# Six small-product groups on TensorE: one matmul of 128 stationary columns, or two of 64

## The chip, the cores and the metric

The kernel runs on one core of a Trainium2 chip. The metric is the device time of one execution in microseconds. The engines are TensorE (PE in the profile, its weight loads PEld), VectorE (DVE), ScalarE (ACT), GpSimd (POOL) and SyncE (SP), which issues nearly all DMAs.

## The reference

Two requests (512 and 256 tokens, width 1024) pass through two layers. In each layer, four mixers (A: grouped-query attention, B: differential attention, C: retention, D: RWKV-7 in both directions) work on one projection of the normalised input, and a SwiGLU feed-forward follows:

```python
for l in range(DEPTH):
    h = _rms(x, p['norm_mix_pre'][l])
    z = h @ p['w_in'][l]
    z_a, z_b, z_c, z_d = jnp.split(z, list(GROUP_OFFS), axis=-1)
    ...
    mix = jnp.concatenate([o_a, o_b, o_c, o_d], axis=-1) @ p['w_out'][l]
    x = x + _rms(mix, p['norm_mix_post'][l])
    h = _rms(x, p['norm_ffn_pre'][l])
    f = (jax.nn.silu(h @ p['ffn_w_gate'][l]) * (h @ p['ffn_w_up'][l])) @ p['ffn_w_down'][l]
    x = x + _rms(f, p['norm_ffn_post'][l])
```

A head is 64 wide. So the product of attention weights with values (A, B, C) has 64 output columns, and D's state is a 64 x 64 matrix for each head and direction.

## The kernel before

Every layer has a mixer phase and a feed-forward phase. The large products (input projection `zc`, `zb`, `zv`, `za`, `dz`, output projection `op`, feed-forward `fg`, `fu`, `dn`) split their operands into a high and a low part of type fp32r and take three matmuls each, with 128 stationary columns (the `lhsT` operand, loaded by LDWEIGHTS) and 256 or 512 moving columns (the `rhs` operand, streamed by MATMUL). The text below calls them the dense matmuls. The small products are plain fp32; the trace holds two MATMUL and two LDWEIGHTS records for each of these.

In the mixer phase, six streams are woven (`weave`): D's preparation and chain, the dense projections, the preparation of heads, the attention units, and the two output stages. The tile framework then orders each engine's instructions by its own timeline of the program (`schedule_with_timeline_sim`), so the order on TensorE is found by a scheduler and not written out by hand. An engine works through its instructions in that order.

These are the small products that the change touches, by the name of the PSUM tile that they write:

- `sd`, in `scores` inside `d_chain` (L537): 64 rows, 128 stationary columns, 128 moving columns. Eight matmuls in each of the 12 chain steps of a layer. The row half (`h`) decides which 64 rows of the array they use.
- `px` and `pg`, in `step_of` inside `d_chain` (L575, L592): 128 rows, 128 stationary and 64 moving columns, eight matmuls each in a chain step. Between them stands `pu` (L584), which already uses 64 rows and 64 stationary columns: rows and columns 0 to 63 for one head, 64 to 127 for the other.
- `oa` and `ob`, in `pv_mm` (L766): probabilities times values of attention A and B, 128 stationary and 64 moving columns, four (first request) or two (second request) matmuls that accumulate.
- `oc`, in `att_c` (L907): the same product for C.

For both layers together these are 192 matmuls each of `sd`, `px` and `pg`, and 160 each of `oa`, `ob` and `oc`. A chain step runs `sd`, masks on DVE, `px`, a copy on ACT (`xy`), `pu`, copies on ACT, `pg`, and state updates on DVE.

Of the kernel before, what the change touches and what calls it, by code (L numbers as in the profile page):

```python
# [19 lines left out]
P = 128  # L20
# [62 lines left out]
class Trunk:  # L83
# [71 lines left out]
    def piece(self, l, idx, n=1024, tags=("whi", "wlo")):  # L155
        nc = self.nc
        raw = self.slot("raw", [P, 1024], f"raw{l}_{idx}")
        nc.sync.dma_start(out=raw[:, :n], in_=self.wp[l, idx][:, :n])
        w = 768 if tags[0] == "D" else 1024
        hi = self.slot(tags[0], [P, w], f"whi{l}_{idx}", F32R)  # L160
        lo = self.slot(tags[1], [P, w], f"wlo{l}_{idx}", F32R)
        nc.scalar.activation(hi[:, :n], raw[:, :n], AF.Copy)  # L162
        self.nlo += 1
        eng = nc.vector if idx in FAST or self.nlo % 2 == 0 else nc.gpsimd
        eng.tensor_tensor(out=lo[:, :n], in0=raw[:, :n], in1=hi[:, :n].bitcast(F32), op=ALU.subtract)  # L165
        return hi, lo

    def tok_mm(self, ps, t, parts, ncol):

# [328 lines left out]
    def d_chain(self, l):  # L498
        nc = self.nc
        V, S, A, T = nc.vector, nc.scalar, nc.gpsimd, nc.tensor  # L500
        H = (slice(0, 64), slice(64, 128))
# [6 lines left out]
        def scores(s, step):  # L508
            t0, n, tt0, ntl, c0, nch = SEQS[s]
            nm = f"{l}_{s}_{step}"  # L510
            chunk = (c0 + step, c0 + nch - 1 - step)
            krs, bks, brs, svs = [], [], [], []
            tt = tta[:, (2 * s + step % 2)]
            for d in range(2):
                c = chunk[d]
                kt, bt = self.tmp(f"kr{nm}_{d}"), self.tmp(f"br{nm}_{d}")
                kr = kt[:, 0:512].rearrange("p (h q x) -> p h q x", h=2, q=2)
                bk = kt[:, 512:768].rearrange("p (q x) -> p q x", q=2)
                br = bt[:, 0:512].rearrange("p (h q x) -> p h q x", h=2, q=2)
                sv = bt[:, 512:768].rearrange("p (h q x) -> p h q x", h=2, q=2)  # L520
                for h in range(2):
                    nc.sync.dma_start(out=kr[H[h], h].rearrange("p q (k x) -> p q k x", k=2), in_=self.kd[d, c, H[h], :, 0:2, :])
                nc.sync.dma_start(out=bk.rearrange("p q (k x) -> p q k x", k=2), in_=self.kd[d, c, :, :, 2:4, :])
                for h in range(2):
                    nc.sync.dma_start(out=sv[H[1 - h], h],
                                      in_=self.vd[c * 64:c * 64 + 64, :].rearrange("t (q h x) -> t q h x", q=2, h=2)[:, :, h, :])
                nc.sync.dma_start(out=tt[:, d], in_=self.td[c, :, d])
                krs.append(kr)
                bks.append(bk)
                brs.append(br)  # L530
                svs.append(sv)

            psv = [self.bank("pb", f"sd{nm}_{h}").rearrange("p (d q x) -> p d q x", d=2, q=2) for h in range(2)]
            for d in range(2):
                for q in range(2):
                    for h in range(2):
                        T.matmul(psv[h][:, d, q], lhsT=bks[d][H[h], q], rhs=krs[d][H[h], h, q], start=True, stop=True)  # L537
            for d in range(2):
                for h in range(2):
                    oh, ot = H[h], H[1 - h]  # L540
                    x, y = (slice(64, 128), slice(0, 64)) if h == 0 else (slice(0, 64), slice(64, 128))
                    V.tensor_tensor(out=krs[d][ot, h], in0=psv[h][ot, d], in1=self.mask[ot, d:d + 1, :].to_broadcast([64, 2, 128]), op=ALU.mult)
                    V.tensor_tensor(out=brs[d][oh, h, :, x], in0=psv[h][oh, d, :, x],
                                    in1=self.mask[oh, d:d + 1, y].to_broadcast([64, 2, 64]), op=ALU.mult)
                    A.memset(brs[d][ot, h, :, x], 0.0)
            pt = self.bank("pb", f"bt{nm}")
            ptv = pt.rearrange("p (d q x) -> p d q x", d=2, q=2)
            for d in range(2):
                for q in range(2):
                    T.transpose(ptv[:, d, q], bks[d][:, q], self.ident)  # L550
            for d in range(2):
                S.activation(brs[d][:, 0, :, 0:64], ptv[:, d, :, 0:64], AF.Copy)
                S.activation(brs[d][:, 1, :, 64:128], ptv[:, d, :, 64:128], AF.Copy)
            return krs, brs, svs, tt

        def step_of(s, step, krs, brs, svs, tt):
            t0, n, tt0, ntl, c0, nch = SEQS[s]
            nm = f"{l}_{s}_{step}"
            ms = sta[:, s]
            msv = ms.rearrange("p (d q) x -> p d q x", q=2)  # L560
            wc = self.wc[:, c0 + max(step, 1) - 1]

            for d in range(2):
                for h in range(2):
                    if step == 0:
                        A.memset(svs[d][H[h], h], 0.0)
                    else:
                        V.tensor_tensor(out=svs[d][H[h], h], in0=msv[H[h], d], in1=wc[H[h], d].unsqueeze(2).to_broadcast([64, 2, 64]),
                                        op=ALU.mult)
            if 0 < step < nch - 1:  # L570
                A.tensor_tensor(out=msv, in0=msv, in1=wc.unsqueeze(3).to_broadcast([P, 2, 2, 64]), op=ALU.mult)
            px = self.bank("pb", f"px{nm}")
            pxv = px.rearrange("p (u x) -> p u x", x=64)
            for u, (h, d, q) in enumerate(units):
                T.matmul(pxv[:, u], lhsT=krs[d][:, h, q], rhs=svs[d][:, h, q], start=True, stop=True)  # L575
            xy = xya[:, s]
            S.activation(xy, pxv, AF.Copy)
            yield 2
            pu = self.bank("pb", f"pu{nm}")
            puv = pu[:, 0:256].rearrange("p (d q x) -> p d q x", d=2, q=2)  # L580
            for d in range(2):
                for q in range(2):
                    for h in range(2):
                        T.matmul(puv[H[h], d, q], lhsT=tt[H[h], d, q], rhs=xy[H[h], 4 * h + 2 * d + q], start=True, stop=True)  # L584
            for d in range(2):
                for h in range(2):
                    S.activation(svs[d][H[h], h], puv[H[h], d], AF.Copy)
            yield 2
            pg = self.bank("pb", f"pg{nm}")
            pgv = pg.rearrange("p (u x) -> p u x", x=64)  # L590
            for u, (h, d, q) in enumerate(units):
                T.matmul(pgv[:, u], lhsT=brs[d][:, h, q], rhs=svs[d][:, h, q], start=True, stop=True)  # L592
            yy = sta[:, 2 + s]
            for h in range(2):
                us = slice(4 * h, 4 * h + 4)
                if step == 0:
                    V.tensor_copy(out=ms[H[h]], in_=pgv[H[h], us])
                elif step < nch - 1:
                    V.tensor_tensor(out=ms[H[h]], in0=pgv[H[h], us], in1=ms[H[h]], op=ALU.add)
            for h in range(2):  # L600
                us = slice(4 * h, 4 * h + 4)
                V.tensor_tensor(out=yy[H[1 - h]], in0=pgv[H[1 - h], us], in1=xy[H[1 - h], us], op=ALU.add)
            for d, c in enumerate((c0 + step, c0 + nch - 1 - step)):
                rows = self.yd[d, c * 64:c * 64 + 64].rearrange("t (q h x) -> t q h x", q=2, h=2)
                for h in range(2):
                    nc.sync.dma_start(out=rows[:, :, h], in_=yy[H[1 - h], 2 * d:2 * d + 2])
            yield 2
# [155 lines left out]

    def pv_mm(self, po, pT, v, nt):
        for j in range(nt):
            self.nc.tensor.matmul(po, lhsT=pT[:, j * P:(j + 1) * P], rhs=v[:, j], start=j == 0, stop=j == nt - 1)  # L766

    def pieces(self, l, idx):
        return [(*self.piece(l, idx + i), range(4 * i, 4 * i + 4), 256, 0) for i in range(2)]
# [119 lines left out]
    def att_c(self, l, g, s):  # L889
        nc = self.nc  # L890
# [3 lines left out]
        w = []  # L894
        for j in range(nt):
            if j % 2 == 0:
                wt = self.slot("Q", [P, 2, 512], f"w{nm}_{j}")
            ps = self.bank("pS", f"s{nm}_{j}")
# [5 lines left out]
        po = self.bank("pO", f"o{nm}")  # L904
        for i in range(nt):
            for j in range(nt):
                nc.tensor.matmul(po[:, i * 64:i * 64 + 64], lhsT=w[j][:, i * P:(i + 1) * P], rhs=z[:, j, 128:192], start=j == 0, stop=j == nt - 1)  # L907
            if i % 2:
                yield 1.5
        pov = po[:, :nt * 64].rearrange("p (i d) -> p i d", d=64)  # L910
# [545 lines left out]
```

## Time and profile before

| | us |
|---|---|
| median of 3 runs | 2338.31 |
| lowest and highest run | 2332.1, 2345.1 |
| the profiled execution | 2336.97 |
| its span, first to last instruction | 2335.2 |
| PE busy in the span | 2246.6 (96%) |
| DVE busy in the span | 1291.8 (55%) |

All times of the trace count from the span's start. Layer 0's mixers end at about 590 us, its feed-forward at about 1160; layer 1's mixers end at about 1760 and its feed-forward closes the span. A PE group is named by line, output tile and inputs, then the part of the array that it uses (rows*columns: 128*128 is all of it, 64*128 half the rows, 64*64 a quarter), then the moving operand's shape. The duration of one MATMUL record includes its way through the array, so records overlap: the pace of a run is read from the starts, not from durations.

### The profile page before, as it was taken

How to read it: one execution, taken by the hardware profiler on the slowest of the kernel's cores; microseconds unless marked ns; L12 is line 12 of the kernel's file. 1: busy time of each engine (PE TensorE's matmuls, PEld its weight loads, DVE VectorE, ACT ScalarE, POOL GpSimd, SP SyncE). 2: the span in 40 equal slices, each digit the busy share in tenths (PEclk: the TensorE clock that was granted, in tenths of full speed). 3: DMA queues.
4: the chain of work that ended last, by engine and by line, in shares of the span. 5: the costliest groups of instructions: out<-in, count | busy, mean ns of one | idle time of the engine just before them, and what ended most of it. 6: DMA issues, size and time to landing. Idle time of an engine off the chain costs nothing.

```text
span 2335.2 us, 39824 instructions
## 1 busy us (share of the span) xinstructions
PE 2246.6 (96%) x15960; PEld 2028.8 (87%) x15960; DVE 1291.8 (55%) x2404; ACT 804.5 (34%) x1675; POOL 582.5 (25%) x521
## 2 busy tenths in 40 slices
PE   7999999999899999999999899999999999999997
PEld 7889999989888888888888799898898888888886
DVE  5598557885623333333567874678855343333345
ACT  4333335566431111221244333455654211222111
POOL 1342313325311111111233422133352111111113
PEclk9999999999999999999999899999999999999999
DMA  4543563335421111222324525633453111122112
GB/s 170 134 113 98 156 193 110 93 113 178 145 79 55 63 55 55 72 73 73 102 87 125 134 78 146 204 104 88 131 189 117 64 63 55 55 73 73 64 64 81
DMA packets 245080, 240.69 MB, mean 103 GB/s; under 512 B 138784, under 2 KB 191904, under 8 KB 244896
## 3 DMA queue, kind: packets, MB, share of 16 engines
q1 hardware_dynamic: 244896, 238.15, 33.2%
q8 instruction: 126, 2.06, 0.4%
q14 instruction: 58, 0.48, 0.1%
HBM read 183.03 MB, written 55.05 MB: 102 GB/s over the span
## 4 chain that ended last, share of the span: by engine, by line
PE 37%; DVE 7%; DMA 2%; issue 1%; ACT 1%; SPq 1%; POOL 1%; DVEq 0%; POOLq 0%; ACTq 0%
PE fg L189 8%; PE fu L189 8%; PE dn L1231 8%; PE dz L189 2%; PE op L178 2%; PE za L178 1%; PE zb L178 1%; PE pg L592 1%; DVE wlo L165 1%; PE px L575 1%; PE ob L766 1%; DMA raw<-in_wp_dram 1%; PE sd L537 1%; PE zc L178 1%; DVE nper L455 1%
## 5 line engine op out<-in xcount | busy, mean ns | idle before, releaser
L165 POOL TENSOR_TENSOR wlo<-raw,whi 128x1024 fp32r<-128x1024 f32 (+1 forms) x108 | 259.4, 2402 | 1034.9 <-ACT whi L162 854.7
L1237 DVE TENSOR_TENSOR y<-y,dn 128x512 f32<-128x512 f32 x240 | 162.7, 686 | 340.4 <-PE dn L1231 339.8
L162 ACT ACTIVATE whi<-raw 128x1024 fp32r<-128x1024 f32 (+1 forms) x222 | 225.3, 1021 | 334.3 <-DMA raw<-in_wp_dram 121.1
L189 PE MATMUL fg<-hh,whi 128*128 128x256 f32 (+1 forms) x768 | 250.4, 326 | 0.9 <-ACT hh L202 0.9
L189 PE MATMUL fg<-hl,whi 128*128 128x256 f32 (+1 forms) x768 | 250.4, 326 | 0.4 <-DVE hl L203 0.4
L189 PE MATMUL fg<-hh,wlo 128*128 128x256 f32 (+1 forms) x768 | 249.2, 325 | 0.0
L189 PE MATMUL fu<-hl,whi 128*128 128x256 f32 (+1 forms) x768 | 249.1, 324 | 0.0
L189 PE MATMUL fu<-hh,whi 128*128 128x256 f32 (+1 forms) x768 | 249.0, 324 | 0.0
L189 PE MATMUL fu<-hh,wlo 128*128 128x256 f32 (+1 forms) x768 | 248.4, 323 | 0.0
L165 DVE TENSOR_TENSOR wlo<-raw,whi 128x1024 fp32r<-128x1024 f32 (+1 forms) x114 | 154.6, 1356 | 128.8 <-ACT whi L162 127.8
L1231 PE MATMUL dn<-whi,ah 128*128 128x512 f32 x528 | 208.9, 396 | 1.9 <-DVE y L1237 1.9
L1231 PE MATMUL dn<-wlo,ah 128*128 128x512 f32 x528 | 209.4, 397 | 0.0
L1231 PE MATMUL dn<-whi,al 128*128 128x512 f32 x528 | 203.8, 393 | 0.0
L189 PEld LDWEIGHTS fg<-hh,whi 128*128 128x128 f32 x768 | 146.4, 191 | 16.1 <-ACT hh L202 1.3
L189 PEld LDWEIGHTS fg<-hl,whi 128*128 128x128 f32 x768 | 146.1, 190 | 15.1 <-DVE hl L203 1.0
L189 PEld LDWEIGHTS fu<-hl,whi 128*128 128x128 f32 x768 | 146.3, 190 | 13.6
L189 PEld LDWEIGHTS fu<-hh,wlo 128*128 128x128 f32 x768 | 146.1, 190 | 13.7
L189 PEld LDWEIGHTS fg<-hh,wlo 128*128 128x128 f32 x768 | 146.3, 190 | 13.4
L189 PEld LDWEIGHTS fu<-hh,whi 128*128 128x128 f32 x768 | 146.4, 191 | 13.1
L1219 ACT ACTIVATE ah<-th 128x768 fp32r<-128x768 f32 (+2 forms) x52 | 38.6, 742 | 297.6 <-DVE th L1217 297.6
L1197 ACT ACTIVATE th<-fg 128x512 f32<-128x512 f32 (+1 forms) x88 | 42.7, 485 | 234.8 <-PE fg L189 234.2
L1231 PEld LDWEIGHTS dn<-whi,al 128*128 128x128 f32 x528 | 98.7, 188 | 23.3
(358 smaller groups left out, 5586.6 us busy)
## 6 DMA issues: line engine op xcount, KB each, us to landing
raw<-in_wp_dram SPq DMA_DIRECT2D x184, 512.0 KB
raw<-in_wp_dram SPq DMA_DIRECT2D x38, 384.0 KB
kr<-kd SPq DMA_DIRECT2D x96, 64.0 KB
kr<-kd SPq DMA_DIRECT2D x48, 128.0 KB
x<-xm SPq DMA_DIRECT2D x24, 256.0 KB
xf<-x SPq DMA_DIRECT2D x12, 512.0 KB
gain<-in_bc_dram SPq DMA_DIRECT2D x8, 512.0 KB
bd<-sh SPq DMA_DIRECT2D x8, 512.0 KB
```

Source lines behind the costliest of these rows:

```text
L162: nc.scalar.activation(hi[:, :n], raw[:, :n], AF.Copy)
L165: eng.tensor_tensor(out=lo[:, :n], in0=raw[:, :n], in1=hi[:, :n].bitcast(F32), op=ALU.subtract)
L178: mm(ps, lhsT=a, rhs=b[:, c:c + ncol], start=i == 0, stop=i == tot - 1)
L189: mm(ps, lhsT=a, rhs=b, start=i == 0, stop=i == 3 * NK - 1)
L455: V.tensor_tensor(out=q[:, j + 1:32, 0:j], in0=q[:, j + 1:32, 0:j], in1=ev, op=ALU.add)
L537: T.matmul(psv[h][:, d, q], lhsT=bks[d][H[h], q], rhs=krs[d][H[h], h, q], start=True, stop=True)
L575: T.matmul(pxv[:, u], lhsT=krs[d][:, h, q], rhs=svs[d][:, h, q], start=True, stop=True)
L592: T.matmul(pgv[:, u], lhsT=brs[d][:, h, q], rhs=svs[d][:, h, q], start=True, stop=True)
L1197: nc.scalar.activation(th[:, c], pg[s][:, :n], AF.Tanh, scale=0.5)
L1219: nc.scalar.activation(ah[:, c], th[:, c], AF.Copy)
L1231: nc.tensor.matmul(ps, lhsT=a[p], rhs=w[q], start=i == 0, stop=i == tot - 1)
L1237: nc.vector.tensor_tensor(out=yt, in0=yt, in1=ps, op=ALU.add)
```

## The change

A new helper issues two matmuls of 64 stationary columns, the first for columns and output partitions 0 to 63, the second for 64 to 127, and the six groups call it in place of one matmul of 128 stationary columns:

```diff
+    def halves_mm(self, ps, lhsT, rhs, start=True, stop=True):
+
+        for c in (slice(0, 64), slice(64, 128)):
+            self.nc.tensor.matmul(ps[c], lhsT=lhsT[:, c], rhs=rhs, start=start, stop=stop)
...
-                        T.matmul(psv[h][:, d, q], lhsT=bks[d][H[h], q], rhs=krs[d][H[h], h, q], start=True, stop=True)
+                        self.halves_mm(psv[h][:, d, q], bks[d][H[h], q], krs[d][H[h], h, q])
...
-                T.matmul(pxv[:, u], lhsT=krs[d][:, h, q], rhs=svs[d][:, h, q], start=True, stop=True)
+                self.halves_mm(pxv[:, u], krs[d][:, h, q], svs[d][:, h, q])
...
-                T.matmul(pgv[:, u], lhsT=brs[d][:, h, q], rhs=svs[d][:, h, q], start=True, stop=True)
+                self.halves_mm(pgv[:, u], brs[d][:, h, q], svs[d][:, h, q])
...
-            self.nc.tensor.matmul(po, lhsT=pT[:, j * P:(j + 1) * P], rhs=v[:, j], start=j == 0, stop=j == nt - 1)
+            self.halves_mm(po, pT[:, j * P:(j + 1) * P], v[:, j], j == 0, j == nt - 1)
...
-                nc.tensor.matmul(po[:, i * 64:i * 64 + 64], lhsT=w[j][:, i * P:(i + 1) * P], rhs=z[:, j, 128:192], start=j == 0, stop=j == nt - 1)
+                self.halves_mm(po[:, i * 64:i * 64 + 64], w[j][:, i * P:(i + 1) * P], z[:, j, 128:192], j == 0, j == nt - 1)
```

In the built program, `px`, `pg`, `oa`, `ob` and `oc` now use the array in the form 128*64 (864 matmuls on columns 0 to 63, 864 on columns 64 to 127), and `sd` in the form 64*64. TensorE has 15108 matmuls in place of 14052. Nothing else in the program's text differs, but the scheduler lays out all engines anew.

The rows below are the order on PE, from the built programs: line, operation, output tile<-inputs, the output's partitions x elements, and how many like it follow each other. In `px_0_5` the numbers are request and chain step. The first place is layer 0, request 0, chain step 5, around `px`; before:

```order
L804 MATMUL tqa_0_0_5166<-cs,xa_0_0_4886 128x128 x4
L575 MATMUL px_0_5_4876<-br_0_5_0_4715,kr_0_5_0_4714 128x64 x2
L575 MATMUL px_0_5_4876<-br_0_5_1_4723,kr_0_5_1_4722 128x64 x2
L575 MATMUL px_0_5_4876<-br_0_5_0_4715,kr_0_5_0_4714 128x64 x2
L575 MATMUL px_0_5_4876<-br_0_5_1_4723,kr_0_5_1_4722 128x64 x2
L537 MATMUL sd_0_6_0_4927<-kr_0_6_0_4911 128x128 x2
L537 MATMUL sd_0_6_0_4927<-kr_0_6_1_4919 128x128 x2
L766 MATMUL ob_1_0_1_4894<-vb_0_3780,pTb_1_0_1_0_5070 128x64 x4
L970 MATMUL sb_1_0_1_3_0_5220<-kb_1_0_1_4515,qb_1_0_1_4514 128x512
```

The same place with the change:

```order
L183 MATMUL za_1_1_0_5787<-wlo_11_5407,hh 128x256
L171 MATMUL px_0_5_5228<-br_0_5_0_5035,kr_0_5_0_5034 64x64 x4
L171 MATMUL px_0_5_5228<-br_0_5_1_5043,kr_0_5_1_5042 64x64 x4
L171 MATMUL px_0_5_5228<-br_0_5_0_5035,kr_0_5_0_5034 64x64 x4
L171 MATMUL px_0_5_5228<-br_0_5_1_5043,kr_0_5_1_5042 64x64 x4
L171 MATMUL sd_0_6_0_5287<-kr_0_6_0_5271 64x128 x4
L171 MATMUL sd_0_6_0_5287<-kr_0_6_1_5279 64x128 x4
L764 MATMUL ptb_1_0_1_1_5609<-cs,pb_1_0_1_1_5366 128x128 x4
L975 MATMUL sb_1_0_1_3_1_5629<-kb_1_0_1_4803,qb_1_0_1_4802 128x512
```

Eight matmuls of `px` have become 16, still in one stretch, but now the form changes three times here (128*128 to 128*64, to 64*64, back to 128*128), where it changed twice (to 64*128 for `sd` and back). The second place is the retention product of head 0, request 1, in layer 0, between dense matmuls `zc`; before:

```order
L178 MATMUL zc_1_1_0_2193<-whi_16_1967,hh 128x256
L476 MATMUL pq_0_1243<-z_0_1147,nt_0_566 32x32
L178 MATMUL zc_1_1_0_2193<-wlo_16_1968,hh 128x256
L178 MATMUL zc_1_1_0_2193<-whi_16_1967,hl 128x256
L907 MATMUL oc_0_1_2219<-zc_0_1_1885,wc_0_1_0_2155 128x64 x4
L178 MATMUL zc_1_1_1_2239<-whi_15_1961,hh 128x256
```

The same place with the change:

```order
L183 MATMUL zc_1_1_0_2241<-whi_16_1999,hl 128x256
L171 MATMUL oc_0_1_2267<-zc_0_1_1917,wc_0_1_0_2203 64x64 x7
L481 MATMUL pq_0_1243<-z_0_1147,nt_0_566 32x32
L171 MATMUL oc_0_1_2267<-zc_0_1_1917,wc_0_1_0_2203 64x64
L183 MATMUL zc_1_1_1_2291<-whi_15_1993,hh 128x256
```

Four `oc` matmuls that stood among dense ones in the same form are now eight in another form, and a `pq` of a third form has moved in between. Counted over the whole order, the form changes 190 times before (94 times away from 128*128 and back, two times between other forms) and 477 times with the change (218 times away from 128*128 and back, 41 times between other forms).

## Rows read from the trace of the kernel before

**Rows 1.** The page, sections 1 and 2: busy us, and tenths in 40 slices.

```profile
span 2335.2 us, 39824 instructions
PE 2246.6 (96%) x15960; PEld 2028.8 (87%) x15960; DVE 1291.8 (55%) x2404; ACT 804.5 (34%) x1675; POOL 582.5 (25%) x521
PEclk9999999999999999999999899999999999999999
```

**Rows 2.** Stretches: length, busy us (instructions) of PE, PEld, DVE, ACT, POOL, clock, DMA.

```profile
160.00:280.00 120.00, 117.22 (x1258) 112.39 (x1257) 83.94 (x210) 42.22 (x104) 31.94 (x55) 0.97 0.42 114
280.00:470.00 190.00, 185.56 (x1615) 175.66 (x1615) 134.44 (x315) 91.93 (x257) 49.41 (x72) 0.97 0.47 137
470.00:590.00 120.00, 110.14 (x877) 105.41 (x876) 81.96 (x189) 73.72 (x185) 47.05 (x43) 0.97 0.47 154
590.00:1160.00 570.00, 563.49 (x3178) 491.81 (x3178) 221.71 (x313) 132.84 (x182) 103.61 (x49) 0.99 0.22 75
1445.00:1635.00 190.00, 184.83 (x1617) 173.30 (x1616) 138.25 (x320) 92.38 (x259) 48.68 (x72) 1.00 0.46 139
```

**Rows 3.** The chain that ended last, by line, from 1520 to 1640 us.

```profile
by line: PE za L178 28.3%; PE pg L592 9.1%; PE ob L766 8.9%; PE px L575 7.5%; PE sd L537 6.4%; PE sb L970 4.9%; PE ptb L759 4.2%; PE pu L584 3.1%; DMA raw<-in_wp_dram 2.6%; issue 2.6%; PE bt L550 1.8%; SPq L606 1.3%; PE oT L1009 1.3%; DVE s
```

**Rows 4.** PE groups by shape: records | busy us, mean ns | idle before, releaser.

```profile
L537 PE MATMUL sd<-kr 64*128 64x128 f32 x384 | 47.4, 288 | 3.0 <-DMA kr<-kd 1.3 <-PE sb L970 0.9 <-issue 0.8
L592 PE MATMUL pg<-br 128*128 128x64 f32 x384 | 46.9, 275 | 0.7 <-ACT br L587 0.7
L575 PE MATMUL px<-br,kr 128*128 128x64 f32 x384 | 46.8, 274 | 0.3 <-DVE br L568 0.3
L766 PE MATMUL oa<-za,pTa 128*128 128x64 f32 x320 | 42.6, 277 | 0.2 <-DVE ob L991 0.2
L766 PE MATMUL ob<-vb,pTb 128*128 128x64 f32 x320 | 42.5, 270 | 0.0
L907 PE MATMUL oc<-zc,wc 128*128 128x64 f32 x320 | 42.0, 270 | 1.7 <-DVE wc L901 1.2 <-DVE oc L917 0.4
```

**Rows 5.** Timeline of PE at one `px` run: start us, us from first start to last end.

```profile
260.18 1.95 PE L575 MATMUL px<-br,kr 128*128 128x64 f32 x16
261.97 0.50 PE L907 MATMUL oc<-zc,wc 128*128 128x64 f32 x3
```

**Rows 6.** Timelines of PE, then PEld, at one `pu` run between dense matmuls.

```profile
272.61 0.28 PE L178 MATMUL zb<-whi,hl 128*128 128x256 f32 x1
272.73 0.28 PE L178 MATMUL zb<-whi,hh 128*128 128x256 f32 x1
272.94 0.68 PE L584 MATMUL pu<-xy,tt 64*64 64x64 f32 x16
273.55 0.39 PE L178 MATMUL zb<-wlo,hh 128*128 128x256 f32 x1
273.77 0.28 PE L178 MATMUL zb<-whi,hl 128*128 128x256 f32 x1
...
272.93 0.55 PEld L584 LDWEIGHTS pu<-xy,tt 64*64 64x64 f32 x16
```

**Rows 7.** The `pu` records: count, duration ns min/median/max, first and last start.

```profile
L584 PE MATMUL pu<-xy,tt x384: 217/218/366, 272.9 to 1631.3; 64*64 64x64 f32 x192
L584 PEld LDWEIGHTS pu<-xy,tt x384: 129/135/228, 272.9 to 1631.3; 64*64 64x64 f32 x192
```

**Rows 8.** Timeline of PE at an `sd` run of one row half, layer 1.

```profile
1573.58 0.28 PE L178 MATMUL za<-wlo,hh 128*128 128x256 f32 x1
1573.79 1.16 PE L537 MATMUL sd<-kr 64*128 64x128 f32 x8
1574.87 0.39 PE L178 MATMUL za<-whi,hl 128*128 128x256 f32 x1
1575.10 0.33 PE L766 MATMUL ob<-vb,pTb 128*128 128x64 f32 x2
```

**Rows 9.** Timeline of PE at an `sd` run whose row halves take turns, layer 0.

```profile
371.95 1.17 PE L537 MATMUL sd<-kr 64*128 64x128 f32 x16
```

**Rows 10.** Stretches as in rows 2, where DVE is busiest.

```profile
400.00:450.00 50.00, 49.52 (x419) 46.69 (x418) 41.11 (x86) 26.94 (x71) 14.81 (x19) 1.00 0.31 88
1550.00:1600.00 50.00, 50.00 (x432) 47.48 (x433) 42.21 (x95) 28.97 (x77) 16.45 (x21) 1.00 0.26 69
```

## The prediction

> **What bounds the kernel now.** I read the totals first: PE is busy for 96% of the span, DVE for 55% [rows 1]. The table of stretches says where that holds. In the mixer stretches that contain the changed products, PE is busy 117 of 120, 186 of 190 and 110 of 120 us in layer 0, and layer 1 is alike (185 of 190 in its chain stretch) [rows 2]. The granted clock is 0.97 to 1.00 there, so nearly all of it is at 2.4 GHz, and no clock term enters the sum. The feed-forward stretch (563 of 570 us) holds none of the six groups and should stay as it is. The chain that ended last confirms that PE's queue sets the pace: from 1520 to 1640 us, `za`, `pg`, `ob`, `px`, `sd`, `sb`, `ptb` and `pu` alone make 72% of it [rows 3]. So time taken from PE in these stretches should mostly come off the end, and time added on PE comes onto it. The reader should look at the six groups next: about 42 to 47 us of busy time each, 268 us together, almost no idle time before them [rows 4]. Busy time counts overlapped pipeline ends, so the price of a matmul has to be taken from starts.
>
> **What one product costs now.** A `px` run of 16 records starts at 260.18, the next run at 261.97: 1.79 us, 112 ns a record, and 223 ns for a matmul of two records [rows 5]. `pg`, `oa`, `ob` and `oc` have the same shape and nearly the same mean and busy time per record [rows 4]. They are 192 + 192 + 3 x 160 = 864 matmuls.
>
> **What two halves cost.** No row shows the form 128*64. The nearest is `pu`: 64 stationary columns, 64 moving ones, on two quarters of the array that differ in rows and in columns [rows 6]. Its 16 records take 0.68 us; the last one lasts 0.22 [rows 7], so 15 steps take 0.46 us, 31 ns a record. Its 16 loads take 0.55 us, the last lasts 0.135, so 28 ns a load. As two quarters take turns, one quarter alone goes at 55 to 62 ns. If the two column halves of `px` work beside each other as `pu`'s quarters do, a former matmul becomes four records of 31 ns, 124 in place of 223 ns. If they go one after the other, it becomes four of about 58 ns, 232: 9 ns more than now. I take the first. What speaks for it is `sd`: where its matmuls stay on one row half, 8 records take 1.16 us [rows 8]; where the halves take turns, 16 records take 1.17 [rows 9]. So parts of the array that share all columns and differ in rows run side by side, and `pu` shows it for parts that differ in both. Parts that share all rows and differ in columns alone are what is not shown.
>
> The Trainium skill speaks on both sides here. "TensorE: Matmul & The Clock Gate", Part 3, "What overlaps and what doesn't", says that a load overlaps running matmuls only when the row group differs; by that the halves of `px` would go in turn and the first term of the sum would be a loss of 8 us. "TensorEngine Tiling (Array Packing)", "Key Properties", says that different tiles load and multiply in parallel, columns included; by that it is the gain taken below. The trace bears out the first page's condition for rows and has no case of columns alone.
>
> **First term:** 864 x (223 - 124) = 86 us less on PE.
>
> **Second term, the changes of form.** A run in another form than its neighbours is not free. Dense matmuls start every 0.12 us. Around `pu`, from the last dense start before (272.73) to the second dense start after (273.77) there are 1.04 us; two dense steps are 0.24 and 16 records are 0.50, so 0.30 us are left for going over and back [rows 6]. (The second start counts, because the first dense matmul after it is recorded at 273.55 and yet holds the next one up by 0.22.) Around the `sd` run the same reckoning gives 1575.10 - 1573.58 = 1.52, less 0.24, less 8 x 0.112: 0.38 us [rows 8]. I take 0.34 for a trip to 128*64 and back, and half of it, 0.17, for a direct change between two other forms. Before, none of the 864 matmuls paid this, since they had the dense form. The order has 218 trips in place of 94 and 41 direct changes in place of two: 124 x 0.34 + 39 x 0.17 = 42 + 7 = 49 us more on PE. By the ends it is 43 to 54 us.
>
> So a run must be long enough to earn its trip. Eight former matmuls (`px`, `pg`) gain 0.79 us and pay 0.34. Four (`oa`, `ob` of the first request) gain 0.40. Two (`oa`, `ob` of the second request, pieces of `oc`) gain 0.20, a loss.
>
> **Third term, `sd`.** Each record still streams 128 moving columns, so its 112 ns stay [rows 8]; the halved load was hidden under that. 192 matmuls become 768 records of which two at least run at once: 43 us, as if all 384 records went singly now. If four quarters run at once, 21 us. Before, some runs already had two row halves at once [rows 9] and most did not. I take 4 us less, with 15 less and 7 more as ends. The masks on DVE, the memsets on POOL, the copies on ACT and all DMAs are the same in number and size. Their cover is the dense matmuls beside them, which stay, and no wait is added.
>
> **Sum.** -86 + 49 - 4 = -41 us of work on PE, about 20 in each layer's mixers. Not all comes off the end: the chain steps pass through ACT and DVE between `px`, `pu` and `pg`, and DVE is at 41 to 42 us of 50 where the attention units run [rows 10]. I let 6 us go there: -35. Against the profiled execution of 2336.97 us (span 2335.2, 1.8 us around it) that is 2302; the median of the runs stands 1.3 us higher, so I say 2303. With trips at 0.30, `sd` at -15 and nothing lost, it is -58 (2280); with trips at 0.38, `sd` at 0 and half lost, it is -16 (2322). These are the forecast's own ends.
>
> **Rivals.**
>
> *The halves go one after the other (slower).* Place: the 128*64 runs. Then the first term is +8 us, the trips remain at +49, and `sd`'s column halves in turn cost 0 to +43, depending on how much its row halves overlap. That is +57 to +100, 2396 to 2438, around 2410. It decides from a pace of 42 ns a record on: 864 x (223 - 4 x 42) is 48 us, just what the trips take. For it: no row shows columns alone side by side, and both halves read the same 128 partitions, for weights and for moving data. Against it: `pu` and `sd` show independent work in every other pairing [rows 6, 9]. Chance 0.18.
>
> *PE gets shorter, the end does not.* DVE at 84% and the chain's latencies take the bound, and the scheduler's new order may open waits of its own. -41 us on PE would turn into idle time before PE's instructions, and the time would be 2327 to 2340. For it: the DVE rows [rows 10]. Against it: PE is at 96% and most of the chain is PE [rows 2, 3]. Chance 0.11.
>
> *Changes between 128*128 and 128*64 are free.* Both `pu` and `sd` change the number of rows too, so their price might not hold for columns alone. Then the 49 us fall away: -90, or 2250. For it nothing but the missing row; against it, both known changes cost 0.30 or more [rows 6, 8]. Chance 0.06.
>
> That the change doesn't do what it says is ruled out as far as the program goes: the built order holds the 1728 matmuls of 128*64.
>
> **How the numbers follow.** Forecast 0.65, the rivals 0.18, 0.11 and 0.06. A measurement of this kernel can tell about 0.5%, 12 us, from no change. Faster by more than that (below 2327): the forecast and the free changes, 0.70, leaving 0.01 of the forecast's far end. Within it: that 0.01 and the second rival, 0.12. Slower: the first rival, 0.18. The range goes from the free changes (2250) to a little above the second rival (2345); left out are the first rival and about 0.02 on the low side.
>
> **What would show it.** A `px` run would have 32 records of the form 128*64 in about 1.0 us, and the chain's `xy` copies would come about 0.8 us sooner after the first `px`; if it takes 1.9 us, the first rival holds. From the last dense start before a 128*64 run to the second after it, 0.3 to 0.4 us should remain when the dense steps and the records are taken off; 0 would be the third rival. `sd` runs of 16 records or more would take no longer than 112 ns for each pair. The stretches from 590 to 1160 and from 1760 on would keep their length, and the mixer phases would each be 15 to 20 us shorter, with PE still at 94% or more; if PE's share falls below that at an unchanged length, it is the second rival. A time above 2345 would mean that the halves do not share the array, and one below 2280 that trips are cheaper, or `sd` far better, than I read.

## The result and the profile after

The changed kernel takes 2308.68 us in the median (2306.99 to 2315.69), the kernel before 2338.8 beside it. The ratio is 0.9877, with a 95% interval from 0.9842 to 0.9912: faster by 1.2%, 30 us, where 35 were forecast (2303, range 2250 to 2345). The profiled execution took 2307.11 us.

The page of the changed kernel, sections 1 and 2, to be read beside [rows 1]:

```profile
span 2305.3 us, 44071 instructions
...
PE 2195.2 (95%) x18072; PEld 1940.4 (84%) x18072; DVE 1278.9 (55%) x2404; ACT 803.9 (35%) x1675; POOL 577.7 (25%) x521
...
PEclk9999999999999999999999999999999999999999
```

PE is busy 2195.2 us in place of 2246.6, so 51.4 less; the span fell by 29.9. The difference, 21.5 us, is new idle time on PE (110.1 in place of 88.6). So the work got cheaper by more than forecast, and less of that reached the end. The clock bears little on this pair: the mean granted clock is 0.979 before and 0.981 after, which is 97 and 89 us at 1.2 GHz, worth at most 4 us of the 51.4.

The phases say where. A mixer phase ends where the feed-forward's first `fg` starts. The two mixer phases of the kernel before, then of the changed kernel, in the columns of [rows 2]:

```profile
0.00:597.60 597.60, 562.76 (x4853) 528.18 (x4854) 416.05 (x905) 276.81 (x668) 180.69 (x206) 0.97 0.46 137
1159.20:1756.40 597.20, 566.30 (x4876) 529.13 (x4875) 426.36 (x890) 272.66 (x660) 195.45 (x211) 0.97 0.44 129
```

```profile
0.00:585.20 585.20, 537.29 (x5909) 484.58 (x5910) 413.85 (x905) 276.32 (x667) 181.16 (x205) 0.97 0.48 140
1145.50:1728.70 583.20, 543.25 (x5932) 486.48 (x5931) 417.55 (x889) 272.55 (x661) 192.70 (x211) 0.96 0.46 132
```

The mixers are 12.4 and 14.0 us shorter, with 25.5 and 23.1 us less PE work; PE's share fell from 94 and 95% to 92 and 93%. Of the 29.9 us, 26.4 came off the mixers and 3.5 off the two feed-forward phases, whose work is the same.

The groups of the changed kernel, which answer to [rows 4]:

```profile
L171 PE MATMUL sd<-kr 64*64 64x128 f32 x768 | 40.3, 281 | 7.2 <-DMA kr<-kd 4.1 <-ACT xy L582 1.4 <-issue 1.0
L171 PE MATMUL ob<-vb,pTb 128*64 128x64 f32 x640 | 31.1, 229 | 0.5 <-ACT pTb L766 0.5
L171 PE MATMUL oa<-za,pTa 128*64 128x64 f32 x640 | 29.7, 232 | 1.2 <-ACT pTa L766 0.9
L171 PE MATMUL oc<-zc,wc 128*64 128x64 f32 x640 | 29.1, 234 | 0.0
L171 PE MATMUL px<-br,kr 128*64 128x64 f32 x768 | 28.0, 224 | 1.2 <-DVE br L573 1.2
L171 PE MATMUL pg<-br 128*64 128x64 f32 x768 | 27.9, 225 | 0.0
```

Twice as many records, and each 128*64 group is busy 28 to 31 us in place of 42 to 47. The timeline of PE in the changed kernel, a `pg` and a `px` run between dense matmuls, and another `px` run with the copy on ACT that waits for it:

```profile
384.50 0.28 PE L183 MATMUL za<-wlo,hh 128*128 128x256 f32 x1
384.70 1.15 PE L171 MATMUL pg<-br 128*64 128x64 f32 x32
385.68 1.10 PE L171 MATMUL px<-br,kr 128*64 128x64 f32 x32
386.72 0.38 PE L183 MATMUL za<-whi,hl 128*128 128x256 f32 x1
386.94 0.28 PE L183 MATMUL za<-whi,hh 128*128 128x256 f32 x1
```

```profile
262.84 1.15 PE L171 MATMUL px<-br,kr 128*64 128x64 f32 x32
...
264.04 0.60 ACT L582 ACTIVATE xy<-px 128x512 f32<-128x512 f32 x1 [0.90 <-PE px L171]
```

From 384.50 to 386.94 there are 2.44 us; less two dense steps of 0.12, 2.20. Runs of 4, 8, 16, 32 and 64 records between dense matmuls in this trace leave 0.46, 0.57, 0.81, 1.27 and 2.21 us by the same reckoning: a straight line of 0.34 us and 29.2 ns a record. So the halves work beside each other (29 ns, not 58), and the trip costs 0.34. The copy `xy` starts 1.20 us after the first `px`. Before, it started 1.99 us after a `px` at 260.18 [rows 5]:

```profile
262.17 0.60 ACT L577 ACTIVATE xy<-px 128x512 f32<-128x512 f32 x1 [1.62 <-PE px L575]
```

What PE waited for in the changed kernel's layer 0 chain stretch, 280 to 470 us (who waits, for whom: us in total, times, longest), largest first, and then the two largest of the kernel before in the same stretch:

```profile
PE tb L940 <- POOL zb L733: 3.9, 1, 3.9
PE ptb L764 <- DVE pb L981: 3.0, 1, 3.0
...
PE tb L940 <- DVE sl L943: 2.3, 1, 2.3
```

```profile
PE ptb L759 <- DVE sl L938: 2.0, 1, 2.0
PE bt L550 <- DVE br L543: 1.1, 1, 1.1
```

The work on DVE, ACT and POOL in the mixers is nearly unchanged (842, 549 and 376 us before, 831, 549 and 374 after), PE has less to do in between, and waits for their results. The waits listed are of that kind; whether an earlier arrival or the new order makes each of them is not separated here. The chain that ended last, 1495 to 1600 us, has more of DVE and POOL in it than before. Added up over all its lines, of which the view shows the first, PE holds 67%, DVE 19% and POOL 6%; in the same stretch of the kernel before they hold 90, 3 and 0%:

```profile
by line: PE za L183 28.0%; PE sd L171 7.4%; PE ob L171 6.6%; PE ptb L764 5.9%; PE pg L171 5.0%; PE sb L975 4.6%; DMA fb<-yd 4.1%; PE px L171 4.0%; PE pu L589 2.4%; issue 2.3%; DVE kr L547 2.2%; POOL ra L151 2.2%; POOL rb L151 2.0%; PE bt L5
```

### The profile page after: what moved, and what is told of

Read it like the earlier page. It is cut to its first block, busy times and chain, and to the rows that moved or that the text cites. A ratio compares the mean times of both kernels' runs of the same rounds, so it can differ in the third digit from the quotient of the medians.

```text
span 2305.3 us, 44071 instructions
## 1 busy us (share of the span) xinstructions
PE 2195.2 (95%) x18072; PEld 1940.4 (84%) x18072; DVE 1278.9 (55%) x2404; ACT 803.9 (35%) x1675; POOL 577.7 (25%) x521
## 4 chain that ended last, share of the span: by engine, by line
PE 37%; DVE 7%; DMA 3%; issue 1%; POOL 1%; ACT 1%; SPq 0%; DVEq 0%; POOLq 0%; ACTq 0%
PE fg L194 8%; PE fu L194 8%; PE dn L1236 8%; PE dz L194 3%; PE op L183 2%; PE za L183 1%; PE zb L183 1%; DVE nper L460 1%; DVE el L458 1%; PE sd L171 1%; DMA bd<-sl 1%; PE zv L183 1%; PE ob L171 0%; DMA fb<-yd 0%; PE pg L171 0%
```

## The experiments

Theory: the gain is the side-by-side work of two column halves, 86 us, less the trips, 49 us, that is, the changes to another form and back. First rival: what helps is only that a load has half the columns, or a new order that happens to be better. Ratios are to the kernel before on the same chip, with the 95% interval; busy and idle times are from each kernel's profiled execution.

### Halves written one after the other

The same matmuls in the same forms, but all products on columns 0 to 63 first, then all on 64 to 127. `pg`, `oa`, `ob` and `oc` are edited like `px`; `sd` stays as changed.

```diff
-            for u, (h, d, q) in enumerate(units):
-                self.halves_mm(pxv[:, u], krs[d][:, h, q], svs[d][:, h, q])
+            for c in (H[0], H[1]):
+                for u, (h, d, q) in enumerate(units):
+                    T.matmul(pxv[c, u], lhsT=krs[d][:, h, q, c], rhs=svs[d][:, h, q], start=True, stop=True)
```

> The changed kernel with the two column halves no longer taking turns: in each run of px, pg, oa, ob and oc all matmuls on columns 0 to 63 come first, then all on columns 64 to 127. The same 1728 matmuls, loads and bytes, 225 trips away from 128*128 in place of 218. Theory (the gain comes from two column halves working side by side): in px and pg, eight matmuls of one half are 16 records at about 58 ns before the other half starts, so most of the overlap is gone; 384 former matmuls lose up to 108 ns, 41 us, and the runs of four lose part of it, 10 to 40 us. Expected 2350 to 2390, slower than before. Rival (the shorter loads or the new order of the schedule bring the gain, not the halves side by side): as the changed kernel, 2300 to 2316.

Measured: 2339.5 us, 1.0015 [1.0001, 1.0028]. The gain is gone. PE is busy 2246.4 us, as much as before the change. The timeline of PE in this kernel, a `pg` and a `px` run between dense matmuls:

```profile
309.59 0.28 PE L183 MATMUL zv<-whi,hh 128*128 128x256 f32 x1
309.80 1.72 PE L599 MATMUL pg<-br 128*64 128x64 f32 x29
...
311.47 0.22 PE L581 MATMUL px<-br,kr 128*64 128x64 f32 x1
311.47 0.22 PE L599 MATMUL pg<-br 128*64 128x64 f32 x1
311.53 1.68 PE L581 MATMUL px<-br,kr 128*64 128x64 f32 x29
313.13 0.39 PE L183 MATMUL zv<-wlo,hh 128*128 128x256 f32 x1
313.36 0.28 PE L183 MATMUL zv<-whi,hl 128*128 128x256 f32 x1
```

309.59 to 313.36, less 0.24, is 3.53 us where the changed kernel takes 2.20, and 16 whole matmuls at 223 ns take 3.57. Less the trip, that is 50 ns a record on average. The time is a miss: 2350 to 2390 was expected. Inside one half the records do start 58 ns apart, as I had put it; but where one half ends and the other begins, three or four records of each alternate (a `pg` and a `px` start at the same 311.47), and in short runs that is most of the run: runs of 8 records leave 0.58 us here, 0.57 in the changed kernel. In the long runs, loads of half the columns alone earn no more than their trip; halves that alternate earn more. The first rival falls, as far as the load goes.

### One part of the change alone

Only `px` and `pg` in halves (the other four groups whole again):

```diff
-                        self.halves_mm(psv[h][:, d, q], bks[d][H[h], q], krs[d][H[h], h, q])
+                        T.matmul(psv[h][:, d, q], lhsT=bks[d][H[h], q], rhs=krs[d][H[h], h, q], start=True, stop=True)
...
-            self.halves_mm(po, pT[:, j * P:(j + 1) * P], v[:, j], j == 0, j == nt - 1)
+            self.nc.tensor.matmul(po, lhsT=pT[:, j * P:(j + 1) * P], rhs=v[:, j], start=j == 0, stop=j == nt - 1)
```

> Only px and pg of the recurrence chain are split; sd, oa, ob, oc as before. 122 trips and 12 direct changes, before 94 and 2. Theory (a matmul gains 0.099 us, a trip costs 0.34 us, a direct change 0.17): 384 x 0.099 = 38 less, 28 x 0.34 + 10 x 0.17 = 11 more, 27 us less work on PE, so 2311 to 2320. Rival (the gain goes with the number of matmuls that are split, trips are cheap): 384 of 864, 44% of the 30 us, 2325.

Measured: 2332.95 us, 0.9992 [0.9974, 1.001]. Missed: no gain in time, though PE is busy 21.7 us less (2224.9). Its idle time is 113.6 us, 25 more than before, in a profiled execution of 2340.28 us, one of the slower of its twelve. One wait and what followed it, on the timeline and in stretches of 10 us of this kernel:

```profile
438.03 1.12 PE L764 MATMUL ptb<-cs,pb 128*128 128x128 f32 x4 [3.96 <-DVE ka L820]
```

```profile
430.00:440.00 10.00, 6.04 (x68) 4.85 (x63) 9.77 (x17) 3.51 (x9) 5.59 (x4) 0.81 0.32 97
440.00:450.00 10.00, 10.00 (x64) 8.79 (x65) 3.93 (x10) 2.73 (x7) 1.61 (x2) 0.50 0.52 167
450.00:460.00 10.00, 10.00 (x51) 8.16 (x50) 6.03 (x14) 4.54 (x14) 1.15 (x1) 0.50 0.01 2
460.00:470.00 10.00, 8.41 (x122) 7.43 (x123) 8.19 (x19) 7.32 (x19) 3.62 (x4) 0.99 0.36 107
```

PE stood 3.96 us behind one `ptb`, waiting for DVE, and then ran at 0.50 of its clock (1.2 GHz) although it was busy 10 of 10 us. A second such stretch follows, from 487 us on. Over the whole span PE ran 124 us at 1.2 GHz, against 97 in the kernel before and 89 in the changed one. The other executions have no trace, but their granted clock is on record: 0.971 to 0.979 here, median 0.975, against 0.979 to 0.989, median 0.983, for the 29 executions of the kernel before beside them. So the lower clock is this kernel's, not that one execution's.

Only `oa`, `ob` and `oc` in halves:

```diff
-                self.halves_mm(pxv[:, u], krs[d][:, h, q], svs[d][:, h, q])
+                T.matmul(pxv[:, u], lhsT=krs[d][:, h, q], rhs=svs[d][:, h, q], start=True, stop=True)
```

and the same for `pg` and `sd`.

> Only oa, ob and oc of the attention units are split; sd, px, pg as before. 202 trips and 32 direct changes, before 94 and 2. Theory: 480 x 0.099 = 48 less, 108 x 0.34 + 30 x 0.17 = 42 more, 6 us less work on PE, so 2326 to 2337, hardly to be told from before. Rival (the gain goes with the number of matmuls): 480 of 864, 56% of the 30 us, 2321 or less.

Measured: 2339.0 us, 1.0017 [1.0005, 1.0028], above the theory's band by 2 us. PE is busy 6.7 us less, where 6 were reckoned, and idle 8.8 more. The short runs do little more than pay for their trips.

All but `sd` in halves (the first two lines of the diff above):

> The changed kernel with sd left whole (128 stationary columns, 64*128). 214 trips and 35 direct changes against 218 and 41. Theory (sd's records stream 128 columns either way, splitting it brings about 4 us, between 15 gained and 7 lost, less 2 us of trips): 2301 to 2324, most likely within 5 us of the changed kernel. Rival (four quarters side by side in sd are a good part of the gain): 2320 to 2330.

Measured: 2316.0 us, 0.9921 [0.99, 0.9942]. Its interval and that of the change (0.9842 to 0.9912) overlap, and PE is busy equally long (2195.0 and 2195.2). The group of whole `sd` in this kernel is busy 40.5 us, the split one 40.3 in the changed kernel:

```profile
L542 PE MATMUL sd<-kr 64*128 64x128 f32 x384 | 40.5, 287 | 5.7 <-DMA kr<-kd 2.7 <-issue 2.2 <-PE zv L183 0.9
```

So splitting `sd` took no measurable work from PE. Whether it gains anything on the end isn't settled.

The parts don't add up: -0.1% and +0.2% alone, -1.2% together. Either a trip's price is not what it seems, or the order that the scheduler finds for each kernel weighs as much as the work saved, by idle time or by the granted clock. The next two groups take price and order apart.

### The price of a trip, measured by itself

To the kernel before, 264 products of 48 columns with zeros are added in the feed-forward, each inside a dense `dn` run, once whole and once in halves. They add zeros to what the run accumulates, and need one more tile of zeros, set once.

```diff
...
+                    if i == 3:
+                        nc.tensor.matmul(ps[:, 0:48], lhsT=self.ident, rhs=self.zz, start=False, stop=False)
...
+                    if i == 3:
+                        for c in (slice(0, 64), slice(64, 128)):
+                            nc.tensor.matmul(ps[c, 0:48], lhsT=self.ident[:, c], rhs=self.zz, start=False, stop=False)
```

> The kernel before, with one more fp32 matmul in each of the 264 accumulations of dn (feed-forward): 128 stationary columns (the identity) times 48 moving columns of zeros, added to the accumulation in its middle, so the output is the same. It has the dense form, so there is no trip. It is the base line for the next kernel. Two records of at most 0.112 us each: 264 x 0.22 = at most 59 us more, and at least 264 x 2 x 0.045 = 24 us where the loads hide behind the dense stream. Expected 2360 to 2397.

> As e4_zero_whole, but the added matmul is two of 64 stationary columns: 264 trips to the form 128*64 and back, in a stretch where PE hardly ever waits. Theory (a trip costs 0.34 us and four records 0.029 us each, and all of it comes onto the end here): 264 x 0.457 = 121 us above the kernel before, 2450 to 2465, and 62 to 97 us above e4_zero_whole. Rival (a change between 128*128 and 128*64 is nearly free): 264 x 0.12 = 31 us above the kernel before, and no slower than e4_zero_whole.

Measured: 2386.77 us, 1.0227 [1.021, 1.0245] whole, within its band; 2446.06 us, 1.0484 [1.0463, 1.0505] in halves, 4 us below its band. The halves cost 59.3 us more than the whole ones, 3 us below the expected 62 to 97, 0.225 us for each product. The whole ones added 52.6 us, 0.199 each, so 0.100 a record (no run shows the 0.045 that the lower end of their expectation takes). With four records of 29.2 ns in place of that, a trip costs 0.225 + 0.199 - 0.117 = 0.31 us. The difference is device time, not a reading of starts, and it lands on the end, since PE is hardly ever idle there (6.5 of 561.6 us in layer 0's feed-forward before) and the clock is level (medians 0.984 before, 0.9835 and 0.9845). The 29.2 ns are taken over from records of 64 columns. The 0.31 agrees with the 0.34 read from the starts to within 10%. The trip's price stands, and the order is left.

### The same kernels in another order

The weave that feeds the scheduler gives its dense streams a rate. Changing it from 1.3 to 1.35 adds and removes no operation; it changes only the order in which the streams are written and so the order that the scheduler finds.

```diff
-D_RATE, DENSE_RATE = 0.5, 1.3
+D_RATE, DENSE_RATE = 0.5, 1.35
```

The kernel before, with this edit:

> The kernel before with DENSE_RATE 1.35 in place of 1.3, a number of the planner alone: about 600 of its 12416 rows of PE's order stand elsewhere, no operation is added or removed (98 trips in place of 94). It measures what another order alone does to the time. Theory (the order in the mixers moves the time by several us either way, which is why the parts of the change do not add up): 2325 to 2350, off from before by 5 us or more. Rival (the order alone does little, and the parts fail to add up for another reason): within 4 us of before.

Only `px` and `pg` in halves, with this edit:

> e5_chain (only px and pg split) with DENSE_RATE 1.35: the same matmuls, 124 trips and 11 direct changes, another order. PE has 27 us less work than before by the prices of a record and a trip. Theory (e5_chain came out level with before because of its order): here part of the 27 us shows, 2308 to 2328. Rival (splitting px and pg alone gains nothing in any order, since the chain waits for other engines then): 2328 to 2340 again.

The whole change, with this edit:

> The whole change with DENSE_RATE 1.35: the same matmuls, 214 trips and 38 direct changes, another order. Theory (the change takes some 50 us of work from PE in any order; how much of it reaches the end depends on the order by about 10 us): 2298 to 2320, 15 to 37 us below the kernel before. Rival (the 1.2% of the change was a lucky order): 2322 to 2335.

Only `oa`, `ob` and `oc` in halves, with this edit:

> e6_att (only oa, ob, oc split) with DENSE_RATE 1.35: 199 trips and 39 direct changes, another order. Theory (the 480 matmuls gain 480 x 0.106 = 51 us and pay 105 x 0.34 + 37 x 0.17 = 42 us for trips, so nearly nothing is left in any order): 2325 to 2340. Rival (e6_att was unlucky in its order as e5_chain was): 2310 to 2322.

Measured, ratio to the kernel before (1.3), with the interval, and PE's busy and idle time in us in the profiled execution; the clock is the median, over all executions, of the mean granted clock:

| halves in | at 1.3 | busy, idle | clock | at 1.35 | busy, idle | clock |
|---|---|---|---|---|---|---|
| none | 1 | 2246.6, 88.6 | 0.983 | 1.0011 [1.0, 1.0022] | 2241.7, 89.9 | 0.983 |
| `px`, `pg` | 0.9992 [0.9974, 1.001] | 2224.9, 113.6 | 0.975 | 0.9957 [0.9941, 0.9974] | 2214.9, 102.2 | 0.981 |
| `oa`, `ob`, `oc` | 1.0017 [1.0005, 1.0028] | 2239.9, 97.4 | 0.982 | 0.9966 [0.9951, 0.998] | 2232.5, 90.0 | 0.985 |
| all six | 0.9877 [0.9842, 0.9912] | 2195.2, 110.1 | 0.9815 | 0.9947 [0.9927, 0.9967] | 2201.3, 127.1 | 0.9775 |

In us the second column of ratios is 2336.3, 2322.79, 2327.99 and 2324.23. The kernel before barely moves (I had thought it would, by 5 us or more), `px` and `pg` alone and `oa`, `ob` and `oc` alone come into the bands expected, and the whole change falls out of the theory's band into that of the rival, a lucky order. At 1.35 the parts together give more (0.4 and 0.3%) than the whole (0.5%). The page of the whole change at 1.35, and what PE waited for in it from 280 to 470 us:

```profile
span 2328.4 us, 44050 instructions
...
PE 2201.3 (95%) x18072; PEld 1947.4 (84%) x18072; DVE 1287.8 (55%) x2404; ACT 806.0 (35%) x1675; POOL 580.7 (25%) x521
```

```profile
PE ptb L764 <- DVE rrb L979: 4.4, 1, 4.4
PE tb L940 <- POOL zb L733: 2.9, 1, 2.9
PE sb L975 <- ACT pb L744: 2.9, 1, 2.9
```

PE is busy 45 us less than in the kernel before here too, but 38.5 us of it stand as idle time in the profiled execution: the same kind of waits as at 1.3, longer. That execution, 2330.19 us, is the slowest of its six, so by the median some 34 us are lost. So the work saved is the change's own and holds in both orders; how much of it reaches the end goes with the order.

Idle time is not the only path from the order to the end. The two kernels of the table in which most of the saved work did not show, `px` and `pg` at 1.3 and all six at 1.35, have its two lowest clocks. Over all executions on record, each set against the mean of its own kernel, a mean clock lower by 0.001 goes with a time longer by 1.4 us (correlation -0.71). By that rate, an estimate, the clock would account for some 11 us of what `px` and `pg` lack at 1.3, and for some 5 of the 16 us between the two orders of the whole change. Which comes first is not shown: a wait can bring the clock down, and a lower clock can lengthen waits, and no run changes one without the other.

### Only the long runs in halves

By the trip's price, runs of two former matmuls lose. This kernel leaves the second request's `oa`, `ob` and `oc` whole:

```diff
+            if nt == 4:
                 self.halves_mm(po, pT[:, j * P:(j + 1) * P], v[:, j], j == 0, j == nt - 1)
+            else:
+                self.nc.tensor.matmul(po, lhsT=pT[:, j * P:(j + 1) * P], rhs=v[:, j], start=j == 0, stop=j == nt - 1)
```

and the same for `oc`, at either rate.

> The whole change, but oa, ob and oc of the second request, which come two matmuls to a run, left whole: 768 split matmuls of that form in place of 864, 186 trips and 35 direct changes in place of 218 and 41. Theory (runs of two pay more for the trip than they gain): 96 x 0.106 = 10 us given up, 32 x 0.34 + 6 x 0.17 = 12 us of trips saved: 2 us less work than the changed kernel, 2300 to 2314. Rival (short runs gain like long ones, the trips of the second request being hidden in waits): 5 us or more slower than the changed kernel, 2313 or more.

> e3_long with DENSE_RATE 1.35: 179 trips and 36 direct changes, the fewest of the versions that split all the long runs. Theory: 4 us less work on PE than the whole change in its own order, 2295 to 2314; the best version if the order is not a worse one. Rival (the other order costs in the attention units what it saved in the chain): 2315 or more.

Measured: 2317.43 us, 0.9927 [0.9906, 0.9948] at 1.3, and 2330.73 us, 0.998 [0.9965, 0.9994] at 1.35. Both are misses, and fall into the rivals' bands; both medians are slower than those of the whole change at the same rate, though the intervals touch. PE is busy 2206.3 and 2199.6 us (2195.2 and 2201.3 with the whole change), so leaving the short runs whole lowered PE's work by no more than 2 us, and idle time is 116.3 and 124.5 us. At 1.3 the rise of 11 us is against the reckoning, which had 2 us less. The granted clock is lower than in the whole change (median 0.980 against 0.9815 at 1.3, and 0.974, the lowest of all, against 0.9775 at 1.35), and idle time is 6 us more at 1.3 and 3 less at 1.35; what makes it end later is not shown. No kernel tried beats the change as made.

## Why the prediction was right, step by step

**What bounds the kernel: right.** The time came out of the mixers, where the changed products stand and PE is busy 94 to 95% of the time, and the feed-forward phases gave 3.5 us of the 29.9 without any change of their work. That no clock term enters the sum held for this pair (0.979 and 0.981); in other orders it did not.

**First term, 86 us less: right.** The four records of a former matmul go at 29.2 ns each, 117 ns in place of the 124 forecast; 864 x (223 - 117) = 92 us. The rows of `pu` [rows 6, 7] were the right neighbours for a form no row showed. The halves written in turn show that this, and not the shorter load, is the gain. The Trainium skill ("TensorE: Matmul & The Clock Gate", Part 3, "What overlaps and what doesn't") says that a load overlaps running matmuls only when the row group differs. The trace here differs: the two halves use the same rows, and a record with its load takes 29.2 ns when halves alternate, 58 within one half when they don't. The measurement decides.

**Second term, 49 us more: right.** 0.34 us per trip, on a straight line from 4 to 64 records, and 0.31 by device time. "TensorEngine Tiling (Array Packing)", "Key Properties", in the Trainium skill says that a change of tiling mode drains the engine, and that tiles run independently. A fixed 0.34 us for each trip agrees with the first, though no row shows a drain as such, and 29.2 ns a record with the second. For the direct changes, taken at 0.17, there is one place by itself, a `pu` run within 128*64 records at 379 us of the changed kernel: with the trip and the records taken off, about 0.20 is left for each.

**Third term, `sd`, 4 us less: not shown.** All four quarters work at once, which is the case for which I had reckoned 21 us in place of 43. A whole `sd` step in the changed kernel, and in [rows 9] half as many records in the same time:

```profile
389.85 1.10 PE L171 MATMUL sd<-kr 64*64 64x128 f32 x32
```

But the whole `sd` takes hardly longer where its row halves take turns: 1.17 us for a step [rows 9], against 1.10. The group's busy time fell by 7.1 us (47.4 to 40.3), and in the kernel that leaves `sd` whole it fell as much, to 40.5. So it came with the new order (41 runs of `sd` before, 34 there, 37 in the changed kernel), and the split itself brought nothing that can be measured. With the measured prices and this 7 the sum is -92 + 49 - 7 = -50, and PE's busy time fell by 51.4.

**What is lost on the way to the end, 6 us: mis-sized.** It is 21.5 us. This is the step that failed. I had read it from DVE's share in two stretches [rows 10], and expected PE's share to stay at 94% or more and each mixer phase to be 15 to 20 us shorter; the share fell to 92 and 93%, and the phases are 12.4 and 14.0 us shorter. A share of an engine doesn't tell how often PE will be at a product before its input is. The two errors, 10 us too little work saved and 15 too little lost, largely cancel: 35 forecast, 30 measured. That they cancel is luck. And the loss is not a constant: at the other rate it was 38.5 us in the profiled execution. A part of the agreement, then, is the order's doing. What both orders share is about 0.5% (0.6% if the kernel before is taken at 1.35 too); the rest of the 1.2% hangs on the order, as far as two orders can show.

**The rivals.** Halves one after the other: excluded by 29.2 ns a record, and the kernel written that way shows its price, 2339.5 us, less than the 2396 I gave, since its halves still overlap where they meet. Free changes of form: excluded by 0.34 and 0.31 us. PE shorter and the end not: its mechanism is there, and took two fifths of the saving; with `px` and `pg` alone it took all of it, with a lower clock beside the waits. Its chance of 0.11 was low for a kernel whose order a scheduler makes.

## What to carry to other kernels

Products like these, fp32 with 64 moving columns, gain when two halves of the stationary columns alternate matmul by matmul, and gained nothing in this kernel when all of one half came first. Products with 128 moving columns on half the rows (`sd`) gained nothing. Reckon a fixed price for each stretch in another form (0.34 us here) and count how many former matmuls a stretch holds: here it takes more than three (0.34 us against 0.106 saved by each). Where a scheduler makes the order, try a change in two or three orders before you trust its size, since the order alone moved these kernels by up to 0.7%, and look at the granted clock beside the idle time.

## What was not expected of the hardware

- The price of a run in another form is a straight line: 0.34 us and 29.2 ns a record, from 4 records to 64.
- Four 64*64 quarters work at once with different rows and columns: 32 records of 128 moving columns in 1.10 us including the last one's tail, against 16 records on two row halves in 1.17 us [rows 9]. For the same products that is no gain.
- After a wait of 3.96 us for DVE, the granted clock was 0.50 (1.2 GHz) in stretches where PE was busy 10 of 10 us, 440 to 460 us in the kernel with only `px` and `pg` in halves. The kernel before had 1.00 from 440 to 450. That this cost the kernel its gain is not shown by a run that changes the clock alone; what speaks for it is that its twelve executions, from 2323.6 to 2342.0 us, have clocks from 0.979 down to 0.971, the longer ones the lower (correlation -0.91).
